# Which queue issues the projection's stores: ScalarE's or SyncE's, in an encoder layer with two kinds of attention

## The chip, the core and the metric

The kernel runs on one NeuronCore of a Trainium2 chip. The metric is the device time of one execution in microseconds. TensorE (PE) multiplies matrices, VectorE (DVE), ScalarE (ACT) and GpSimd (POOL) do the elementwise work, and SyncE (SP) computes nothing: its queue issues DMAs. Every engine takes its instructions in order; an instruction that waits holds all that stand behind it on the same engine.

## The reference

One layer on x of 2048 tokens by 1024 features, float32. A projection gives queries, keys and values of 16 heads of width 64, and 8 forget gates. Eight heads attend causally with a bias of summed log gates; eight attend within their own chunk of 64 tokens and the 8 chunks before, with a bias on clipped distance. The heads' outputs go through a second projection, are added to the input and normalised; then comes a feed-forward part with a causal convolution of width 3 and a gated GELU, and a second normalisation.

```python
proj = x @ w_in
q_a, k_a, v_a, f_a, q_b, k_b, v_b = jnp.split(proj, SPLITS, axis=-1)
y_a = forgetting_attention(split_heads(q_a, N_HEADS_A), split_heads(k_a, N_HEADS_A),
                           split_heads(v_a, N_HEADS_A), log_f)
y_b = chunked_band_attention(split_heads(q_b, N_HEADS_B), split_heads(k_b, N_HEADS_B),
                             split_heads(v_b, N_HEADS_B), rel_bias)
...
x = layer_norm(DEEPNORM_ALPHA * x + mix, ln1_g[l], ln1_b[l])
u = x @ w_up
u = sum(u_pad[:, j:j + s, :] * conv_w[j] for j in range(CONV_WIDTH)) + conv_b
value, gate = jnp.split(u, 2, axis=-1)
return (value * jax.nn.gelu(gate)) @ w_down
```

## The kernel before

Dense products are made of three matmuls each (`mm3`, lines 184 to 186): an operand is split into a high part that the matmul unit represents and a low part that is the rest (`split`, ACT at line 177 and VectorE or GpSimd at line 180). The products of the feed-forward part go by sums and differences of blocks, seven products in place of eight, so their weights have to be summed and split too.

There are four stages. First the projection (`projection`): for each pair of heads `p`, for queries and for keys, and for each of four chunks of 512 tokens, `queries_or_keys` accumulates eight products of 128 by 512, ScalarE writes the high part (line 419), VectorE the low part (line 420), and both are stored to DRAM (lines 423 and 424). `values` does the same for four heads at a time, in blocks of 128 tokens: ScalarE copies the sum (line 399), line 400 stores it. Each of the two functions hands back control after every product of three matmuls: 1024 such units in all, 8 to each of the 128 results.

Attention reads these arrays back. A unit of attention is one head and one chunk of 512 queries. `load_keys` loads kb, ka and vv (lines 514 to 523), `maxima` loads qa and qb (lines 552 to 554, two buffers each), multiplies them (`sc`, line 574), takes maxima on VectorE (lines 577 and 582), and ScalarE copies their transposed row into qb (line 592). `logits` then multiplies again (`st`, lines 611 and 612), ScalarE takes the exponential (line 623), and four steps later `weigh` multiplies by the values (`y`, line 698). The maxima of one unit are made while the unit before it is under way.

`weave` emits projection and attention in turn: so much dense work after each step of attention. Within the dense work, every ninth unit after the 60th takes one step of the generator `prepare_weights`. It loads raw tiles of the second projection's and of the last product's weights (`w_raw`, line 288), sums and splits them (`w_hl`, lines 279, 177, 180) and stores both parts (line 282), so that later stages load them ready. The raw tiles have one buffer each, and so has `w_hl`.

All DMAs are issued by SP. The second projection, the normalisation (until about 1460 us) and the feed-forward part follow.

Of the kernel before, what the change touches and what calls it, by code (L numbers as in the profile page):

```python
# [25 lines left out]
CH = 512  # L26
# [53 lines left out]
    ((7,), (), ((0, 1), (1, 1))),  # L80
)

PRE0, PRE = 60, 9
AHEAD_L, AHEAD_P, RESERVE = 5, 2, 16
DLY_V, DLY_R, DLY_Z = 32, 16, 16
WNEXT = 3
# [13 lines left out]
def f32(ap):  # L100
    return ap.bitcast(F32)
# [3 lines left out]
def hymba_layer(  # L105
# [18 lines left out]
    nc = tc.nc  # L124

    def tl(pool, shape, dt, tag, bufs=None):
        return pool.tile(shape, dt, tag=tag, name=tag, bufs=bufs)
# [46 lines left out]
    def split(hi, lo, src, hi_eng, lo_eng):  # L174

        if hi_eng is nc.scalar:
            nc.scalar.activation(hi, src, AF.Copy)  # L177
        else:
            hi_eng.tensor_copy(hi, src)
        lo_eng.tensor_tensor(lo, src, f32(hi), op=ALU.subtract)  # L180

    def mm3(acc, wh, wl, mh, ml, first, last, **more):

        nc.tensor.matmul(acc, wh, mh, start=first, stop=False, **more)  # L184
        nc.tensor.matmul(acc, wh, ml, start=False, stop=False, **more)  # L185
        nc.tensor.matmul(acc, wl, mh, start=False, stop=last, **more)  # L186
# [57 lines left out]
    def part(ws, k):  # L244
        ks = slice(k % (KT // 2) * P, (k % (KT // 2) + 1) * P)
        return [w[:, ks] for w in ws[k // (KT // 2)]]
# [24 lines left out]
    def prepare_weights(pool):  # L271

        def parts(dst, u, v=None, op=None):
            hl = tl(pool, [P, 2, CH], F32R, "w_hl")
            if v is not None:
                src = f32(hl[:, 1])
                nc.vector.tensor_tensor(src, u, v, op=op)
                u = src  # L280
            split(hl[:, 0], hl[:, 1], u, nc.scalar, nc.vector)
            nc.sync.dma_start(dst.rearrange("l p m -> p l m"), f32(hl))

        def load(src, tiles):
            raws = []
            for n, (i, j) in enumerate(tiles):
                raws.append(tl(pool, [P, CH], F32, f"w_raw{n}"))
                nc.sync.dma_start(raws[n], src[i * P : i * P + P, CH * j : CH * j + CH])
            return raws

        for k in range(0, KT, 2):
            tiles = [(k + n // 2, n % 2) for n in range(4)]
            raws = load(w_out, tiles)
            yield
            for raw, (i, j) in zip(raws, tiles):
                yield
                parts(wo_d[i, j], raw)
        HF = NF // 2
        for k in range(HF):
            raws = load(w_down, [(HF * i + k, j) for i in range(2) for j in range(2)])  # L300
            yield
            for n in DOWN:
                yield
                (k0, l0), v, op = DOWN[n][3:6]
                parts(wd_d[k, n], raws[2 * k0 + l0], v and raws[2 * v[0] + v[1]], op)


    def projection(mem, banks, state):
# [3 lines left out]
        def flush():  # L312
            while pending:
                pending.pop(0)()
# [9 lines left out]
        def gates(c, f):  # L324

            z, u, e, l = (tl(small, [P, TQ, 8], F32, f"gate{n}") for n in range(4))
            nc.vector.tensor_tensor(z, f, bf_t, op=ALU.add)
            nc.vector.scalar_tensor_tensor(u, z, -1.0, z, op0=ALU.mult, op1=ALU.min)
            nc.scalar.activation(e, u, AF.Exp)
            nc.vector.tensor_scalar(u, e, 1.0, None, op0=ALU.add)  # L330
            nc.scalar.activation(l, u, AF.Ln)

            nc.vector.scalar_tensor_tensor(e, u, -1.0, e, op0=ALU.add, op1=ALU.subtract)
            nc.vector.reciprocal(u, u)
            nc.vector.tensor_mul(e, e, u)
            nc.vector.tensor_sub(l, l, e)

            nc.vector.scalar_tensor_tensor(l, z, 0.0, l, op0=ALU.min, op1=ALU.subtract)
            nc.vector.tensor_scalar(l, l, -1.0, None, op0=ALU.mult)
            pending.append(lambda: sums_of_gates(c, l))  # L340
# [42 lines left out]
        def values(g, chunks, vs):  # L383
            nv = 264 if g == 0 else 256
            for c in chunks:
                if g == 0:
                    f = tl(small, [P, TQ, 8], F32, "f", 2)
                for t in range(TQ):
                    o = slice(t * P, t * P + P)
                    acc = banks.get()  # L390
                    for k in range(KT):
                        mm3(acc[:, :nv], *(x[:, o] for x in xs[k, c]), *vs[k], k == 0, k == KT - 1)
                        yield 0.33
                    if t == 1:
                        flush()
                    if g == 0:
                        nc.vector.tensor_copy(f[:, t], acc[:, 256:264])
                    tile = mem.get()
                    nc.scalar.activation(tile[:, :256], acc[:, :256], AF.Copy)
                    nc.sync.dma_start(  # L400
                        v_d[4 * g : 4 * g + 4, :, TQ * c + t, :].rearrange("h p d -> p h d"),
                        tile[:, :256].rearrange("p (h d) -> p h d", d=HD),
                    )
                    mem.put(tile, delay=DLY_E)
                if g == 0:
                    gates(c, f)
            mem.put(*held)
            held.clear()

        def queries_or_keys(p, j, c, ws):  # L410
            hd, ld = ((qh_d, ql_d), (kh_d, kl_d))[j]
            acc = banks.get()
            for k in range(KT):
                mm3(acc, *part(ws, k), *xs[k, c], k == 0, k == KT - 1)
                yield 0.65
            flush()
            hi, lo = mem.get(F32R), mem.get(F32R)
            sc = SCALE if j == 0 else 1.0
            nc.scalar.activation(hi, acc, AF.Copy, scale=sc)
            nc.vector.scalar_tensor_tensor(  # L420
                lo, acc, sc, f32(hi), op0=ALU.mult, op1=ALU.subtract
            )
            nc.sync.dma_start(hd[p, :, c * CH : (c + 1) * CH], f32(hi))
            nc.sync.dma_start(ld[p, :, c * CH : (c + 1) * CH], f32(lo))
            mem.put(hi, lo, delay=DLY_E)

# [2 lines left out]
        for half in range(2):  # L429
# [8 lines left out]
            for g in range(4):  # L438
                for p in (2 * g, 2 * g + 1):
                    if half == 0 and p == 0:  # L440

                        ahead = None
                        for c in chunks:
                            for j in range(2):
                                if (j, c) == (1, 1):
                                    mem.put(*sum(first[0], ()))
                                    ahead = weights(w_qk[1, 0], mem)
                                yield from queries_or_keys(p, j, c, first[j])
                        mem.put(*sum(first[1], ()))
                        continue  # L450
                    for j in range(2):
                        ws = ahead or weights(w_qk[p, j], mem)
                        if (p % 2, j) == VAT:
                            vs = value_weights(g, state.pop("early", None))
                        ahead = None
                        if len(mem.free) >= WFREE + (20 if (p % 2, j) < VAT else 0):
                            ahead = weights(w_qk[(2 * p + j + 1) // 2 % NP, (j + 1) % 2], mem)
                        for c in chunks:
                            yield from queries_or_keys(p, j, c, ws)
                        mem.put(*sum(ws, ()))  # L460
                        if (p % 2, j) == VPOS:
                            yield from values(g, chunks, vs)
# [750 lines left out]
    with ExitStack() as st:  # L1213
# [75 lines left out]
        with ExitStack() as inner:  # L1289
            state["weights"] = prepare_weights(inner.enter_context(tc.tile_pool(name="w_s", bufs=1, side="right")))  # L1290
            with tc.tile_pool(name="v_s", bufs=1, side="right") as state["early"]:
                projected(1)
            pools = attention_pools(inner)
            weave(attention(pools, [0, 1], lambda p: projected(p // 2 + 1)), dense, RATE1)
            weave(attention(pools, [2, 3], lambda p: projected(4 + p // 2 + 1)), dense, RATE2)
# [98 lines left out]
```

## Time and profile before

| | |
|---|---|
| median of 3 runs | 2788.2 us (2786.32 to 2790.31) |
| the profiled execution | 2789.79 us, span 2788.0 us |
| mean granted clock of TensorE | 0.993 |
| busy share of the span: TensorE, VectorE, ScalarE, GpSimd | 98%, 70%, 42%, 22% |

The span reaches from the first to the last instruction of the profiled execution. Times in views are us from the span's start. A wait is given with the instruction that waits, what released it, the sum of such waits, their number and the longest one. "PEld" is TensorE's load of the stationary operand, which runs beside the matmul before it; "q" after an engine's name means its queue of issues and waits.

### The profile page before, as it was taken

Reading aid. Unit: us, or ns where it says so; the run is one execution under the profiler, and the core shown is the slowest. Engines: PE = TensorE matmul, PEld = TensorE weight load, DVE = VectorE, ACT = ScalarE, POOL = GpSimd, SP = SyncE. Lnnn points to the kernel's source line nnn. Section 1 sums busy time; section 2 is a strip of 40 time slices with the busy share of each in tenths; the row PEclk is TensorE's granted clock in tenths of the full one; section 3 lists DMA queues with packets and bytes.
Section 4 is the critical chain, followed back from the end, with each engine's and each line's share of the span. In section 5 each row is a group of like instructions: output and inputs, shape, how many; then the busy total and the mean of one; then the engine's idle time right before and its main releaser. Section 6 shows DMA issues by size and latency. Waiting matters only on the chain.

```text
span 2788.0 us, 38642 instructions
## 1 busy us (share of the span) xinstructions
PE 2724.5 (98%) x12632; PEld 2045.3 (73%) x12632; DVE 1941.7 (70%) x3577; ACT 1160.7 (42%) x2004; POOL 623.2 (22%) x754
## 2 busy tenths in 40 slices
PE   9999999999999999999998999999999999999998
PEld 7676767675666656766786888888887788888886
DVE  4557576777677655668568888876568877777559
ACT  4434444444444443433225555553222555544221
POOL 2235242327567555333000000000000000000000
PEclk9999999999999999999999999999999999999999
DMA  8666767665455444677894444428778222236974
GB/s 242 197 207 196 228 194 229 211 201 169 144 182 182 137 144 153 199 198 217 293 328 142 141 166 156 155 83 311 260 247 322 87 80 81 78 88 206 323 227 161
DMA packets 324618, 527.40 MB, mean 189 GB/s; under 512 B 70688, under 2 KB 86176, under 8 KB 324416
## 3 DMA queue, kind: packets, MB, share of 16 engines
q1 hardware_dynamic: 324416, 524.93, 59.1%
q8 instruction: 100, 1.64, 0.2%
q14 instruction: 102, 0.84, 0.1%
HBM read 362.65 MB, written 162.14 MB: 188 GB/s over the span
## 4 chain that ended last, share of the span: by engine, by line
PE 84%; DVE 4%; DMA 4%; ACT 1%; issue 1%; POOL 0%; SPq 0%; DVEq 0%; ACTq 0%; POOLq 0%
PE acc L184 21%; PE acc L186 21%; PE acc L185 21%; PE y L698 8%; PE st L611 4%; PE sc L574 4%; PE st L612 3%; DMA qb<-qh_d 1%; PE sc L650 1%; DVE slot L180 1%; DVE slot L1132 1%; DMA slot<-in_w_v_dram 1%; DMA wd_d<-w_hl 1%; PE acc L841 0%; DVE slot L816 0%
## 5 line engine op out<-in xcount | busy, mean ns | idle before, releaser
L184 PE MATMUL acc<-slot,slot 128*128 128x512 f32 (+2 forms) x3064 | 1165.7, 381 | 17.9 <-ACT slot L177 17.9
L186 PE MATMUL acc<-slot,slot 128*128 128x512 f32 (+2 forms) x3064 | 1160.5, 379 | 6.6 <-DVE slot L180 6.6
L185 PE MATMUL acc<-slot,slot 128*128 128x512 f32 (+2 forms) x3064 | 1161.3, 379 | 0.0
L177 ACT ACTIVATE slot<-slot 128x512 fp32r<-128x512 f32 (+1 forms) x680 | 416.4, 626 | 674.2 <-DVE slot L1121 193.0
L184 PEld LDWEIGHTS acc<-slot,slot 128*128 128x128 f32 x3064 | 580.4, 189 | 135.9 <-ACT slot L177 23.5
L186 PEld LDWEIGHTS acc<-slot,slot 128*128 128x128 f32 x3064 | 579.7, 189 | 126.2 <-DVE slot L180 10.8
L185 PEld LDWEIGHTS acc<-slot,slot 128*128 128x128 f32 x3064 | 580.4, 189 | 112.6 <-issue 2.8
L180 DVE TENSOR_TENSOR slot<-slot,slot 128x512 fp32r<-128x512 f32 (+1 forms) x652 | 450.7, 707 | 194.4 <-ACT slot L177 167.9
L632 POOL TENSOR_TENSOR sums<-sums,pt 128x512 f32<-128x512 f32 (+3 forms) x416 | 426.0, 1024 | 251.9 <-ACT pt L623 189.0
L623 ACT ACTIVATE pt<-st 128x512 f32<-128x512 f32 (+3 forms) x544 | 261.7, 492 | 333.4 <-PE st L612 121.4
L698 PE MATMUL y<-pt,vv 128*64 128x512 f32 (+3 forms) x1088 | 281.6, 505 | 0.2 <-DVE yt L640 0.2
L611 PE MATMUL st<-qa,ka 128*128 128x512 f32 (+2 forms) x544 | 209.0, 385 | 9.0 <-ACT pt L623 8.5
L574 PE MATMUL sc<-kb,qb 66*128 66x512 f32 (+2 forms) x544 | 186.6, 373 | 10.8 <-DMA qb<-qh_d 8.1
L612 PE MATMUL st<-qb,kb 97*128 97x512 f32 (+2 forms) x544 | 189.9, 357 | 4.4 <-ACT qb L592 3.9
L577 DVE TENSOR_REDUCE mx<-sc 128x1 f32<-128x512 f32 x192 | 127.9, 686 | 80.0 <-PE sc L574 78.3
L611 PEld LDWEIGHTS st<-qa,ka 128*128 128x128 f32 x544 | 103.0, 189 | 96.0 <-issue 44.1
L698 PEld LDWEIGHTS y<-pt,vv 128*64 128x64 f32 x1088 | 82.0, 136 | 124.2 <-issue 111.5
L574 PEld LDWEIGHTS sc<-kb,qb 66*128 66x128 f32 x544 | 99.5, 190 | 78.6 <-DVE mx L582 17.5
L856 DVE SCALAR_TENSOR_TENSOR v<-u,cw,v 128x1024 f32<-128x1024 f32 x88 | 113.0, 1285 | 62.4 <-ACT v L855 44.2
L1005 POOL COPY u<-halo 128x2 f32<-128x2 f32 x44 | 17.6, 401 | 620.8 <-DVE v L857 620.8
L582 DVE CUSTOM_DVE_ANT_0 junk<-sc,bq 128x512 bf16<-128x512 f32 (+2 forms) x224 | 108.2, 483 | 49.4 <-PE sc L574 40.2
L632 POOL TENSOR_TENSOR sums<-pt 128x384 f32<-128x384 f32 (+1 forms) x64 | 79.5, 1243 | 255.4 <-PE sc L650 181.4
(116 smaller groups left out, 2250.3 us busy)
## 6 DMA issues: line engine op xcount, KB each, us to landing
slot<-wd_d SPq DMA_DIRECT2D x308, 256.0 KB
slot<-in_w_up_dram SPq DMA_DIRECT2D x176, 256.0 KB
wd_d<-w_hl SPq DMA_DIRECT2D x77, 512.0 KB
slot<-wo_d SPq DMA_DIRECT2D x128, 256.0 KB
h_d<-v SPq DMA_DIRECT2D x44, 512.0 KB
slot<-h_d SPq DMA_DIRECT2D x88, 256.0 KB
slot<-in_w_qk_dram SPq DMA_DIRECT2D x66, 256.0 KB
xq_d<-slot SPq DMA_DIRECT2D x56, 256.0 KB
```

Source lines behind the costliest of these rows:

```text
L177: nc.scalar.activation(hi, src, AF.Copy)
L180: lo_eng.tensor_tensor(lo, src, f32(hi), op=ALU.subtract)
L184: nc.tensor.matmul(acc, wh, mh, start=first, stop=False, **more)
L185: nc.tensor.matmul(acc, wh, ml, start=False, stop=False, **more)
L186: nc.tensor.matmul(acc, wl, mh, start=False, stop=last, **more)
L574: nc.tensor.matmul(sc[:, m0:m1], qb[:KR, tq], kb[:KR, m0:m1], start=True, stop=True)
L577: nc.vector.tensor_reduce(m, sc[:, k0:k1], axis=AX.X, op=ALU.max)
L611: nc.tensor.matmul(st[:, w2], ka[:, js], qa[:, w2], start=True, stop=False)
L612: nc.tensor.matmul(st[:, w2], kb[:KM, js], qb[:KM, w2], start=False, stop=True)
L623: nc.scalar.activation(pt[:, w], st[:, w], AF.Exp)
L632: nc.gpsimd.tensor_tensor(acc[:, w], (acc if first is None else first)[:, w], pt[:, w], op=ALU.add)
L698: nc.tensor.matmul(y[half, w], v, pt[:, w], start=first and n < 2, stop=last and n >= len(tiles) - 2)
```

## The change

The stores of high parts (line 423) and of values (line 400) are issued by ScalarE's queue in place of SP's. In `prepare_weights`, a group of raw tiles is loaded after one more step of the generator, and the generator takes a step every 8 units in place of 9. The store of low parts (line 424), the loads and all arithmetic stay as they were.

```diff
-PRE0, PRE = 60, 9
+PRE0, PRE = 60, 8
...
         for k in range(0, KT, 2):
             tiles = [(k + n // 2, n % 2) for n in range(4)]
+            yield
             raws = load(w_out, tiles)
             yield
...
         for k in range(HF):
+            yield
             raws = load(w_down, [(HF * i + k, j) for i in range(2) for j in range(2)])
             yield
...
                     nc.scalar.activation(tile[:, :256], acc[:, :256], AF.Copy)
-                    nc.sync.dma_start(
+                    nc.scalar.dma_start(
                         v_d[4 * g : 4 * g + 4, :, TQ * c + t, :].rearrange("h p d -> p h d"),
...
-            nc.sync.dma_start(hd[p, :, c * CH : (c + 1) * CH], f32(hi))
+            nc.scalar.dma_start(hd[p, :, c * CH : (c + 1) * CH], f32(hi))
             nc.sync.dma_start(ld[p, :, c * CH : (c + 1) * CH], f32(lo))
```

## Rows read from the trace of the kernel before

**Rows 1.** The page, busy time of the engines (share, instructions).
```profile
PE 2724.5 (98%) x12632; PEld 2045.3 (73%) x12632; DVE 1941.7 (70%) x3577; ACT 1160.7 (42%) x2004; POOL 623.2 (22%) x754
```
**Rows 2.** Busy time by stage; last: granted clock, DMA share, GB/s.
```profile
94.00:1180.00 1086.00, 1062.15 (x5332) 726.86 (x5331) 704.49 (x1622) 473.13 (x933) 501.62 (x511) 0.99 0.61 185
...
1460.00:2788.00 1328.00, 1302.00 (x5606) 1050.32 (x5604) 1008.54 (x1410) 566.68 (x842) 45.98 (x128) 0.99 0.53 175
```
**Rows 3.** What TensorE's matmuls waited for, 94 to 1180 us: sum, number, longest.
```profile
PE sc L574 <- DMA qb<-qh_d: 8.1, 8, 2.1
PE st L611 <- ACT pt L623: 6.4, 7, 2.1
PE st L612 <- ACT qb L592: 3.9, 3, 2.8
```
**Rows 4.** Busy time around two long waits, and in a stretch between.
```profile
130.00:160.00 30.00, 27.18 (x133) 19.54 (x131) 19.54 (x40) 12.35 (x24) 15.79 (x15) 0.94 0.59 180
160.00:340.00 180.00, 179.79 (x972) 131.41 (x972) 106.65 (x241) 76.06 (x154) 61.92 (x67) 1.00 0.71 214
...
740.00:780.00 40.00, 37.87 (x205) 27.03 (x205) 22.78 (x41) 16.28 (x31) 20.22 (x17) 0.96 0.41 129
```
**Rows 5.** What SP's queue waited for, 0 to 1180 us.
```profile
SPq L423 <- ACT slot L419: 87.3, 47, 6.8
SPq L400 <- ACT slot L399: 69.7, 47, 8.4
SPq L552 <- PE st L612: 59.3, 28, 7.9
...
SPq L424 <- DVE slot L420: 18.3, 32, 2.4
SPq L288 <- DVE w_hl L279: 17.0, 9, 3.5
```
**Rows 6.** The issues of lines 423 and 400, 94 to 1180 us: ns min/median/max, first and last start.
```profile
L423 SPq DMA_DIRECT2D kh_d<-slot x28: 320/327/808, 113.8 to 1178.7; - x28
...
L400 SPq DMA_DIRECT2D v_d<-slot x56: 359/376/539, 160.5 to 1159.6; - x56
```
**Rows 7.** SP's issues in order of time, 744 to 754 us: start, duration.
```profile
745.25 0.38 SPq L400 DMA_DIRECT2D v_d<-slot  x1
...
750.93 0.45 SPq L552 DMA_DIRECT2D qa<-ql_d  x1
...
752.61 0.55 SPq L554 DMA_DIRECT2D qb<-qh_d  x1
```
**Rows 8.** What SP's queue waited for, 745 to 754 us.
```profile
SPq L400 <- ACT slot L399: 8.4, 1, 8.4
SPq L552 <- PE st L612: 3.4, 1, 3.4
SPq L230 <- DMA v_d<-slot: 1.5, 1, 1.5
```
**Rows 9.** A high part, qb's copy and the logits in order of time, 229 us.
```profile
229.29 0.60 ACT L419 ACTIVATE slot<-acc 128x512 fp32r<-128x512 f32 x1 [3.30 <-PE acc L186]
...
229.98 0.59 ACT L592 ACTIVATE qb<-sc 1x512 fp32r<-1x512 f32 x1
...
230.62 0.30 PEld L612 LDWEIGHTS st<-qb,kb 97*128 97x128 f32 x2 [0.25 <-ACT qb L592]
```
**Rows 10.** ScalarE's groups, 94 to 1180 us: busy, mean ns, idle before, releasers.
```profile
L623 ACT ACTIVATE pt<-st 128x512 f32<-128x512 f32 (+1 forms) x468 | 229.5, 501 | 278.2 <-PE st L612 113.8 <-DVE st L621 72.0 <-DVE st L618 57.2
...
L592 ACT ACTIVATE qb<-sc 1x512 fp32r<-1x512 f32 x55 | 32.2, 586 | 45.4 <-PE sc L591 44.9
```
**Rows 11.** What TensorE's weight loads waited for, 94 to 1180 us.
```profile
PEld st L611 <- ACT pt L623: 30.0, 54, 2.5
...
PEld st L612 <- ACT qb L592: 10.3, 16, 3.3
```
**Rows 12.** The stores of prepared weights: ns min/median/max, first and last start.
```profile
L282 SPq DMA_DIRECT2D wd_d<-w_hl x77: 359/377/1182, 208.5 to 1020.1; - x77
```

## The prediction

> **What bounds the kernel now.** I read the page first, then a table by stage, then who waited for whom on TensorE, on SP's queue and on ScalarE, and last the order of single instructions around a store. The page shows TensorE busy for 2724.5 of 2788.0 us [rows 1]: it idles 63.5 us in all, and whatever the other engines and queues do is worth time only where it makes or ends one of those idle stretches. The diff touches the projection, which is woven with attention, and the weight preparation that runs inside it. By stage, that is the stretch from 94 to 1180 us (and the 94 us before it): there TensorE is busy 1062.15 of 1086 us, so 23.85 us are idle; from 1460 us on nothing is touched [rows 2]. The waits that TensorE names in this stretch are 8.1 us for the load of qb (8 times), 6.4 us for an exponential on ScalarE (7 times) and 3.9 us for ScalarE's copy into qb (3 times) [rows 3]; these three are 18.4 of the 23.85 us. The rest is small waits for VectorE and GpSimd, and gaps too short for a releaser.
>
> A long idle stretch costs twice. Around the 2.8 us wait of 130 to 160 us [rows 3, 4] the granted clock is 0.94 of 2.4 GHz on the mean, in the quiet stretch after it 1.00, around the 2.1 us wait for qb at 758 us it is 0.96 [rows 4]. 0.06 of 30 us is 1.8 us, 0.04 of 40 us is 1.6 us: each stall of about 2 us cost about 1.7 us more in clock. Five such dips lie between 94 and 1200 us (two are shown), some 8.7 us by that price. So everything that the change can win in its stretch is some 24 us of idle time and 9 us of clock, 1.2% of the span; a measurable gain needs a sixth of it. For this kernel 0.2%, 5.6 us, is about what a measurement can tell from no change.
>
> **The stores, seen from SP.** 128 issues leave SP's queue: 64 of high parts, 64 of values. In the stretch they are 55 and 56, and one takes 0.327 or 0.376 us on the queue [rows 6] (the 27 stores of qh_d repeat the row of kh_d). SP also stops waiting for ScalarE: 87.3 us before high parts, 69.7 us before values, nearly all that these waits amount to [rows 5]. What is late next?
>
> For high parts nearly nothing is won. The low part's store stands right behind, stays on SP, and waits for a VectorE instruction that itself reads the high part; SP waits for it 18.3 us now, after having waited for the high part, and will wait the whole time then. Only the 0.33 us of issue comes free. I cost this at nothing; its cover is the low part's wait, and without that cover it would be a share of the next item.
>
> For values SP does get free, 69.7 us earlier in sum. Behind them on SP stand the loads of the next attention unit, of weights, and the stores of prepared weights. The stretch before the 2.1 us stall at 758 us is the test, as the longest wait of a value store lies in it: SP waited 8.4 us for ScalarE and issued the store at 745.25; but the load of qa, the first of the three loads that the unit needs, then waited another 3.4 us for a matmul of the unit before, that still read the buffer, and went out at 750.93, qb at 752.61 [rows 7, 8]. The store was gone 5 us before; without it the load goes out at 750.93 all the same. Of SP's waits before qa, 59.3 us, in 28 waits, are for that matmul [rows 5]. So the three loads are held by TensorE's own order and by the buffer, not by the stores. Bounds: nothing, and all of the 8.1 us for qb with the two clock dips at such stalls (1.8 and 1.6), 11.5 us. I take 1 us, one of the eight waits at their mean, near the lower end since the row that should show the link shows the other cause.
>
> By the Trainium skill, page Perfetto Trace Analysis, section DMA Optimizations, one engine may be given the inputs and another the outputs "to allow more dynamic spread"; by it the loads would start earlier, and the sum would go toward the 11.5 us. The row at 745 to 753 us speaks against it for this kernel [rows 7, 8], and no run before shows two issuing engines.
>
> **The stores, seen from ScalarE.** No DMA is issued by ScalarE before, so the nearest rows are the same issues on SP: 55 x 0.327 + 56 x 0.376 = 39 us of ScalarE's queue in the stretch, on an engine that is busy 473 of 1086 us there [rows 2, 6]. What stands behind the store on ScalarE is the next exponential, the copy into qb, or a split of a weight. At 229 us the copy into qb starts 0.09 us after the high part's copy ends, and the weight load of the logits waits for it [rows 9]: an issue in between goes straight to TensorE, 0.33 us.
>
> How often is that so? 468 exponentials and 55 copies into qb feed the logits [rows 10], and 54 + 16 = 70 times the weight load of the logits waited for one of them, 40.3 us [rows 11]: 13% of the 523 end just when they are needed. If each of the 111 stores delays one such instruction, 111 x 0.13 = 15 hits of about 0.35 us are 5.2 us: the upper end. Of the 40.3 us of weight-load waits only 10.3 us are waits of the matmul itself [rows 3]; the rest ran beside a matmul under way. With that share, 0.26, the hits cost 1.4 us: the lower end. I take 3 us, between them: not every store delays an exponential, but the case at 229 us is a full hit. A gain is excluded here: ScalarE gets work and loses none.
>
> **Raw tiles one step later, a step every 8 units.** Each group of four loads now comes after one more step, so the generator has 4 x 6 + 11 x 9 = 123 steps where it had 4 x 5 + 11 x 8 = 108; 1024 - 60 units of the projection give 107 turns every 9 and 120 every 8. The same 93 parts are prepared with the same instructions, at nearly the same pace. SP's waits before the raw loads (17.0 us for VectorE [rows 5]) shrink. No matmul of this stretch reads these weights; the work that hides them is the projection itself: the last store of prepared weights goes out at 1020.1 us and the last key store at 1178.7 [rows 6, 12]. A delay of up to 158 us is covered. If that cover were gone, the three or four steps left at the end would run in one burst, against one or two. I take nothing, with the same bounds as SP's share above.
>
> **Sum.** 2789.79 us was the profiled execution's own time, span 2788.0. +3 on ScalarE, -1 on SP, 0 for the raw tiles: 2791.8. The median of the runs, 2788.2, is 1.6 us below that execution, so 2790 us is what I expect of a median: 0.1% slower, inside what can be told from no change.
>
> **The rivals.**
> *Likeliest, 0.43: a wash.* As summed, 2783 to 2794.
> *SP's freedom reaches TensorE, 0.26: faster.* The loads of qb land earlier at half of the eight waits (4 us) and the two long ones drop below the length at which the clock fell (3.4 us): 2788.2 - 7.4 = 2781. For it speak 69.7 us of SP's waits before value stores, and 17.0 before raw tiles; against it the waits for TensorE behind them, 59.3 us [rows 5], and the case at 745 us. It decides from three or four of the eight on. The page's rule on inputs and outputs is this rival.
> *ScalarE becomes the late one, 0.31: slower.* All 15 hits come at full price, 5.2 us, and three stalls for an exponential or for qb's copy grow into the length that cost clock, 3 x 1.8: 10.6 us, 2799. For it speak that ScalarE already ends 10.3 us of TensorE's waits, and that an issue can also be held by an earlier DMA's landing (1.5 us for a load of w_qk at line 230 [rows 8]), which would then hold the exponentials too; against it that ScalarE idles 56% of the stretch. It decides from the first dip more than before.
> *The change does nothing to the queue* is not a separate case: low parts hold SP as long as high parts did, which is in the sum.
>
> **Numbers.** Faster by over 0.2% (below 2782.6): 0.25, nearly all of the second case. Within: 0.44. Slower (above 2793.8): 0.31. The likeliest case alone is 2783 to 2794; the range reaches into both others, whose centres are 2781 and 2799, to 2778 and 2801: beyond lie the bound of 11.5 us of gain, and more than three added dips.
>
> **What the profile of the changed kernel would show.** SP's waits at the stores of high parts and values are gone; its wait at the low part's store grows from 18.3 us toward 90. If the sum is right, TensorE idles 24 to 28 us from 94 to 1180 us, its waits for ScalarE (10.3 us) grow by 1 to 5, its waits for qb stay within 2 us of 8.1, and the clock is below 0.97 in about as many places. Faster is right if the waits for qb fall below 5 us and the dip at 740 to 780 us is gone. Slower is right if ScalarE's next instruction after a store is what the logits wait for, with more than 15 us of such waits. The prediction is wrong if the engines' orders come out so different that stalls move to other tiles, POOL's sums or VectorE's maxima, by more than 5 us: then the balance of two queues was not the question.

## The result, and the profile after

The changed kernel takes 2805.9 us (median of 8 runs, 2795.9 to 2809.3) against 2787.0 us (2783.5 to 2791.9). The ratio on record is 1.0056, 95% interval 1.0043 to 1.0068; the two medians alone would give 1.0068, its upper end. It is slower, and the median is past the upper end of the predicted range, 2801. The profiled execution spans 2807.5 us. Lines beyond 300 moved by two: the logits are lines 613 and 614, the high part's copy and store 421 and 425, the value's 401 and 402, the low part's store 426, qb's load 556.

The page of the changed kernel, busy time and DMA queues (packets, MB, share of 16 engines); busy time by stage; what TensorE's matmuls waited for from 94 to 1180 us; what SP's queue waited for from 0 to 1180 us; and the two moved stores from 94 to 1180 us (ns min/median/max, first and last start):

```profile
PE 2728.3 (97%) x12632; PEld 2045.0 (73%) x12632; DVE 1934.1 (69%) x3577; ACT 1162.8 (41%) x2004; POOL 620.6 (22%) x754
...
q1 hardware_dynamic: 281408, 499.76, 55.7%
q10 hardware_dynamic: 43008, 25.17, 2.9%
```
```profile
94.00:1180.00 1086.00, 1051.76 (x5230) 715.31 (x5230) 685.22 (x1589) 461.61 (x911) 494.01 (x505) 0.99 0.57 178
1460.00:2788.00 1328.00, 1310.27 (x5645) 1056.78 (x5644) 1004.50 (x1400) 570.90 (x846) 44.86 (x128) 0.99 0.54 177
```
```profile
PE sc L576 <- DMA qb<-qh_d: 13.1, 20, 1.4
PE st L613 <- ACT pt L625: 7.9, 11, 1.5
PE sc L576 <- DVE mx L584: 5.2, 1, 5.2
PE sc L652 <- POOL sums L634: 2.6, 1, 2.6
PE st L614 <- ACT qb L594: 2.1, 3, 1.3
```
```profile
SPq L282 <- DVE w_hl L180: 103.2, 48, 9.0
SPq L426 <- DVE slot L422: 64.4, 37, 7.9
SPq L554 <- PE st L614: 60.4, 24, 8.8
...
SPq L525 <- DMA v_d<-slot: 20.2, 8, 4.1
```
```profile
L425 ACTq DMA_DIRECT2D qh_d<-slot x28: 326/327/353, 95.5 to 1129.4; - x28
```
```profile
L402 ACTq DMA_DIRECT2D v_d<-slot x55: 366/367/431, 160.6 to 1177.4; - x55
```

The stores did move: queue 10, which the kernel before does not use, carries 25.17 MB, and an issue takes 0.327 or 0.367 us on ScalarE, nearly as it did on SP [rows 6]. TensorE is busy 1051.76 of 1086 us from 94 to 1180 us, so it idles 34.2 us where it idled 23.9 [rows 2]. Over the whole span the same 12632 matmuls are busy 3.8 us longer (2728.3 against 2724.5 [rows 1]), so 15.7 of the 19.5 us between the two spans are idle time. From 94 to 1180 us the waiting for qb grew most, from 8.1 us (8 times) to 13.1 (20 times) [rows 3]. One stall for a maximum on VectorE is 5.2 us long, and one for sums on GpSimd 2.6; in the kernel before the same two waits were:

```profile
PE sc L574 <- DVE mx L582: 2.4, 2, 1.2
PE sc L650 <- POOL sums L632: 1.4, 1, 1.4
```

The waits for ScalarE's exponentials and copies into qb, where the price was expected, are 10.0 us, after 10.3. SP waits for low parts 64.4 us (18.3 before [rows 5]), for VectorE's prepared weights 103.2 us (57.3 before), and for landings of the moved stores 71.0 us in 33 waits, all rows that name kh_d, qh_d or v_d as written summed, where it was 13.1 us in 13. Two of these rows in the kernel before:

```profile
SPq L282 <- DVE w_hl L180: 57.3, 28, 7.8
...
SPq L523 <- DMA v_d<-slot: 2.6, 2, 1.9
```

Where the time went can be read by counting exponentials: the 101st of the 544 starts 3.4 us later than before, the 141st 12.4, the 201st 17.4, the 321st 21.3, the last 18.4 us. So the loss is made while attention runs beside the projection, mostly between 345 and 640 us, and little comes on top later. That stretch, first in the changed kernel, then in the kernel before:

```profile
345.00:640.00 295.00, 279.29 (x1434) 197.70 (x1433) 200.98 (x532) 125.33 (x261) 95.71 (x135) 0.98 0.65 199
```
```profile
345.00:640.00 295.00, 286.48 (x1491) 203.72 (x1489) 214.32 (x554) 133.18 (x273) 101.25 (x134) 1.00 0.70 210
```

VectorE and ScalarE get less done there too: all wait more, and the granted clock is 0.98 in place of 1.00. These are two single executions, and the runs of the kernel before lie up to 8.4 us apart, so a difference of a few us in such rows can be chance.

One thing had not been in the prediction's sum. The order in which instructions stand on an engine's queue is not that of the code: a planner fixes it when the kernel is built. Taking 128 stores off SP changes that plan on other engines too. In the two traces that differ only in who issues the stores (the changed kernel and e1_raw_only below), of 120 splits into slots on ScalarE (mostly weights and tokens, line 177) that stand among the exponentials 63 stand further ahead and 7 further behind, 2.7 exponentials earlier on the mean; of 88 splits of prepared weights 87 stand earlier, 15 exponentials on the mean.

One such place. ScalarE's order in the changed kernel, with TensorE's beside it, and below them the same split (the third and the fourth exponential are the same ones too) in e1_raw_only:

```profile
367.69 1.08 ACT L625 ACTIVATE pt<-st 128x512 f32<-128x512 f32 x2 [0.98 <-DVE st L620]
370.88 0.63 ACT L177 ACTIVATE slot<-slot 128x512 fp32r<-128x512 f32 x1 [2.10 <-DMA qh_d<-slot]
371.42 0.54 ACT L625 ACTIVATE pt<-st 128x128 f32<-128x128 f32 x2
```
```profile
370.00 0.28 PE L614 MATMUL st<-qb,kb 97*128 97x256 f32 x1
371.73 0.45 PE L613 MATMUL st<-qa,ka 128*128 128x384 f32 x1 [1.45 <-ACT pt L625]
```
```profile
356.93 1.09 ACT L625 ACTIVATE pt<-st 128x512 f32<-128x512 f32 x2
358.34 0.28 ACT L625 ACTIVATE pt<-st 128x128 f32<-128x128 f32 x1 [0.32 <-PE st L614]
359.43 0.63 ACT L177 ACTIVATE slot<-slot 128x512 fp32r<-128x512 f32 x1 [0.81 <-DMA qh_d<-slot]
359.96 0.75 ACT L625 ACTIVATE pt<-st 128x256 f32<-128x256 f32 x2
```

In e1_raw_only three exponentials are done before the split. In the changed kernel two are; the split then waits 2.10 us until an earlier store has left the slot that it writes, the third exponential waits behind it, and TensorE idles 1.45 us. No store stands between them.

### The profile page after: what moved, and what is told of

Its sections match the earlier page's. It is cut to its first block, busy times and chain, and to the rows that moved or that the text cites. A ratio compares the mean times of both kernels' runs of the same rounds, so it can differ in the third digit from the quotient of the medians.

```text
span 2807.5 us, 38622 instructions
## 1 busy us (share of the span) xinstructions
PE 2728.3 (97%) x12632; PEld 2045.0 (73%) x12632; DVE 1934.1 (69%) x3577; ACT 1162.8 (41%) x2004; POOL 620.6 (22%) x754
## 3 DMA queue, kind: packets, MB, share of 16 engines
q10 hardware_dynamic: 43008, 25.17, 2.9%
## 4 chain that ended last, share of the span: by engine, by line
PE 83%; DMA 8%; DVE 4%; ACT 2%; issue 1%; SPq 1%; POOL 0%; ACTq 0%; DVEq 0%; POOLq 0%
PE acc L186 21%; PE acc L184 21%; PE acc L185 21%; PE y L700 8%; PE sc L576 4%; PE st L613 4%; DMA qb<-qh_d 3%; PE st L614 3%; PE sc L652 1%; DVE slot L180 1%; DMA slot<-in_w_qk_dram 1%; DMA slot<-y_d 1%; DVE slot L1134 1%; DMA qh_d<-slot 1%; DVE slot L818 1%
## 5 line engine op out<-in xcount | busy, mean ns | idle before, releaser
L180 DVE TENSOR_TENSOR slot<-slot,slot 128x512 fp32r<-128x512 f32 (+1 forms) x652 | 444.0, 698 | 203.7 <-ACT slot L177 173.3
L700 PE MATMUL y<-pt,vv 128*64 128x512 f32 (+3 forms) x1088 | 275.9, 507 | 0.0
L658 DVE RECIPROCAL row<-row 128x128 f32<-128x128 f32 x128 | 115.6, 928 | 27.0 <-ACT row L654 26.9
```

The costliest lines, as they stand in the source:

```text
L700: nc.tensor.matmul(y[half, w], v, pt[:, w], start=first and n < 2, stop=last and n >= len(tiles) - 2)
```

## The experiments

Three theories. **ScalarE:** its time for the issues delays exponentials (the prediction's +3 us). **SP:** set free, it runs on into other waits and issues other transfers at other times, and loads come late. **Order:** the new plan of all engines is the loss, whoever issues the stores. Times are ratios to the kernel before on the same chip, with 95% intervals. The expectations use letters: A is a part of the SP theory (loads held by the landing of stores), B lays the loss on the raw tiles' new pace, C is ScalarE, D is order; "queue theories" are SP and ScalarE together. Where two edits are alike, only one of them is printed.

### One part alone

**e1_raw_only**: the raw tiles and the step of 8, the stores left on SP.
```diff
-PRE0, PRE = 60, 9
+PRE0, PRE = 60, 8
...
+            yield
             raws = load(w_out, tiles)
...
```


> Only the raw tiles' extra step and the step every 8 units; all stores stay on SP. Theory A (the stores are the cause: loads that SP could reach earlier are held by the landing of stores that ScalarE issues later): 2787 us, within 4 us of the kernel before, waits for qb near 8 us. Theory B (the prepared weights' new pace, with everything reordered by it, is the cause): 2800 to 2808 us.


Measured 1.0005 [0.9991, 1.0019]: the raw tiles cost nothing that can be measured.

**e2_hi_only**: only the high parts' stores on ScalarE. **e3_v_only**: only the values'. **e4_both_stores**: both, with the raw tiles as before.
```diff
-            nc.sync.dma_start(hd[p, :, c * CH : (c + 1) * CH], f32(hi))
+            nc.scalar.dma_start(hd[p, :, c * CH : (c + 1) * CH], f32(hi))
```


> Only the high parts' stores on ScalarE. Theory A: half of the loss, 2793 to 2800 us. Theory B: 2787 us, within 4 us of before. Theory C (ScalarE's own 0.35 us for each issue delays the exponentials and the copies into qb): about half of the loss too, but with the added idle time at those two, not at the loads of qb.

> Only the values' stores on ScalarE. Theory A: more than half of the loss, 2795 to 2803 us, with SP's waits for the landing of value stores above 50 us (72 us with the whole change, 15 before). Theory B: 2787 us, within 4 us. Theory C: about half of the loss, at the exponentials.

> Both stores on ScalarE, the prepared weights as before. Theory A and theory C: nearly the whole loss, 2800 to 2808 us. Theory B: 2787 us, within 4 us.


Measured 1.0109 [1.0092, 1.0126], 1.0080 [1.0065, 1.0095] and 1.0114 [1.0097, 1.0132]. Either half costs nearly what both cost: no sum over stores does that, neither ScalarE's time per issue nor SP's freedom per store. And e4_both_stores with the raw tiles later is the changed kernel, 1.0056: the raw tiles, which cost nothing alone, give half of the loss back. TensorE's waits in e2_hi_only, 94 to 1180 us:

```profile
PE st L611 <- ACT pt L623: 15.3, 14, 2.4
PE sc L574 <- DMA qb<-qh_d: 11.5, 14, 2.4
```

Against 6.4 and 8.1 us before, both grew, and mostly not after stores: of the 20 gaps of TensorE (21.0 us, before 1220 us) that an exponential or qb's copy ended, four (3.3 us) have a store's issue on ScalarE within the 2.5 us before the gap's end.

### First attempts at the queues

**f1_double**: SP keeps all stores; ScalarE also stores the same tiles to a place that nobody reads.
```diff
             nc.sync.dma_start(hd[p, :, c * CH : (c + 1) * CH], f32(hi))
+            nc.scalar.dma_start(h2_d[j, p, :, c * CH : (c + 1) * CH], f32(hi))
```


> SP keeps all its stores as before, and ScalarE issues the same 128 stores again, into scratch arrays that nobody reads: ScalarE bears the whole of its new work (some 45 us of issues), 25 MB more are moved, and the weights' splits stand in ScalarE's order where they stood before (mean shift 0.0 and -0.7 exponentials). Theory C (ScalarE's time for the issues): 2805 to 2822 us. Theory D (with the stores off SP, the order made for the engines puts the weights' splits 3 to 17 exponentials earlier on ScalarE, and there they wait for loads that on the chip land no earlier, with the exponentials held behind them): within 6 us of 2788.


1.0178 [1.0155, 1.0202]. ScalarE's order is nearly that of before, but 25 MB more move, so this did not separate what it was meant to.

**f2_pool**: GpSimd issues the stores (`nc.gpsimd.dma_start` in both places).


> The same two stores off SP, but issued by GpSimd. ScalarE issues nothing; the splits stand as early as with the stores on ScalarE (2.9 and 17.8 exponentials). Theory C: within 6 us of 2788, or the loss is on GpSimd's sums. Theory D: 2805 to 2822 us, with TensorE's added waits at the exponentials, the copy into qb and the loads of qb.


1.0187 [1.0168, 1.0206]. Nothing is issued by ScalarE, and the loss is greater. But GpSimd takes longer for an issue:

```profile
L423 POOL DMA_DIRECT2D qh_d<-slot x28: 540/557/567, 94.6 to 1155.8; - x28
```
```profile
L400 POOL DMA_DIRECT2D v_d<-slot x50: 750/767/775, 160.6 to 1170.1; - x50
```

and its queue holds attention's sums and the low parts of the values' weights behind the stores, so this too is mixed. ScalarE's order shifts as in e4_both_stores.

**f3_sp_later**: the stores stay on SP, and the code emits them some units of the projection later, so that SP should not have to wait for ScalarE.
```diff
+                if k == LATE:
+                    write()
```


> All stores stay on SP but are emitted three units after their result, so that SP no longer waits for ScalarE and VectorE before them; the splits keep their places (0.0 and 0.0). The rival that forecast a gain from SP's freedom: 2776 to 2783 us. Theory D: SP's freedom is worth little by itself, 2782 to 2790 us, with SP's waits before the stores down from 175 us to under 60.


1.0005 [0.9993, 1.0017], but SP's waits before the stores stayed, 81.9 and 72.4 us (87.3 and 69.7 before [rows 5]): a later place in the code did not make SP issue them later. The attempt says nothing on what SP's waits are worth; it shows that the order on the queue is not the order of the code.

**f4_late_weights**: e4_both_stores with the prepared weights begun later.
```diff
-PRE0, PRE = 60, 9
+PRE0, PRE = 150, 8
```


> Both stores on ScalarE; the prepared weights begin 90 units later and then take a step every 8 units, which puts their splits back to about where they stood (-2.1 exponentials for -16.9), while the splits of the projection's own weights stay 3.1 early. Theory D: a third or more of the loss of 32 us is gone, 2797 to 2810 us. Theory C: 2815 to 2822 us as with both stores on ScalarE.


1.0110 [1.0088, 1.0131]: with the splits of prepared weights back near their old places among the exponentials (2.6 earlier on the mean, 19.2 in e4_both_stores), the loss is the same, as the ScalarE theory would have it. Their early place is not the cause.

### ScalarE's time and issues alone

**g1_act_time**: a second copy of 128x256 behind each of the 128 copies. **g2_tiny**: a store of one row by ScalarE behind each. SP keeps all stores; the order stays nearly as before. The first adds copies that nobody reads, the second 128 small transfers.
```diff
             nc.scalar.activation(hi, acc, AF.Copy, scale=sc)
+            nc.scalar.activation(idle, f32(hi)[:, :256], AF.Copy)   # g1_act_time
+            nc.scalar.dma_start(t_d[j, p, c], f32(hi)[0:1])         # g2_tiny
```


> Stores stay on SP; ScalarE gets, right behind each of the 128 copies, another copy of 128x256 into a tile that nobody reads (0.38 us each by the row of the value copy, 49 us in all, about the time of the 128 issues). It adds ScalarE's time without a DMA. The prediction's price for ScalarE's time: +1.4 to +5.2 us, 1.0005 to 1.002. If ScalarE's time is the whole loss of e4_both_stores: 1.008 to 1.013. If it costs nothing: 0.999 to 1.001.

> Stores stay on SP; ScalarE also issues, behind each of the 128 copies, a store of one row (1 or 2 KB) of the same tile to a place that nobody reads: the same number of issues, order of the engines nearly as before, hardly any bytes. If the issue on ScalarE with its queue's own handling is the loss: 1.008 to 1.013. If f1_double (1.0178) lost by its 25 MB of added traffic and by landings: 1.000 to 1.004.


0.9990 [0.9977, 1.0003] and 0.9988 [0.9978, 0.9998]. In g1_act_time ScalarE (the fourth busy time) is busy 512.72 us where it was 473.13 [rows 2], and TensorE, the first, loses 2 us of busy time in that window:

```profile
94.00:1180.00 1086.00, 1060.14 (x5322) 724.70 (x5321) 706.83 (x1621) 512.72 (x1042) 499.75 (x511) 0.99 0.61 185
```

The ScalarE theory falls as an account of the loss: 40 us more work, or 128 more issues, cost nothing that can be measured. The order was not held here, only nearly kept, so a gain by a slightly other plan could hide a loss of 0.1 or 0.2%.

### The order held

`add_manual_dep` with NoSync ties an instruction behind another of its own engine without a wait. With one such edge between each two neighbours, the five queues can be given the order that another kernel has (all but the moved stores, which the planner places):
```python
for a, b in zip(names, names[1:]):          # one engine's instructions, in the wanted order
    tc.add_manual_dep(
        by[b], a,
        mybir.DependencyInfo(mybir.DependencyClass.NoSync, mybir.DependencyReason.DATA),
        reason="order",
    )
```
**h1_order_alone**: stores on SP, all queues in the order of e4_both_stores. **h2_queue_alone**: stores on ScalarE, all queues in the order of the kernel before. **i1_after_order** and **i2_after_queue**: the same two for the changed kernel and e1_raw_only.

> Stores stay on SP as in the kernel before, but every engine's instructions (on SP: all but the moved stores) are held, by edges that order and do not wait, in the order that they have in e4_both_stores (1.0114). Order theory (the plan that the two queues bring about, with splits of weights earlier on ScalarE, ahead of exponentials, is the loss): 1.008 to 1.014, waits for exponentials and for qb together 25 us or more. Queue theories (the loss is in what the queues do at run time: SP free to walk into other waits, landings of stores on another queue, ScalarE's issue time): 0.998 to 1.004, the two waits together under 20 us.

> Both stores on ScalarE as in e4_both_stores, but every engine's instructions (on SP: all but the moved stores) are held in the order that they have in the kernel before. Order theory: 0.997 to 1.003, the waits for exponentials and qb together back at 13 to 20 us. Queue theories: 1.008 to 1.014 with 25 us or more of the two waits; ScalarE's issue time at the price of the prediction alone (+3 us, at most 5.2): 1.000 to 1.002.

> The change itself in place of e4_both_stores: raw tiles as in the changed kernel, stores on SP (e1_raw_only: 1.0005), every engine's instructions held in the order that they have in the changed kernel. Order theory: 1.006 to 1.014, waits for exponentials and qb together 22 us or more; theory of two about equal causes, order and queue, in the changed kernel (1.0056): 1.002 to 1.005; queue alone: 0.998 to 1.002.

> The changed kernel (stores on ScalarE, raw tiles later), with every engine's instructions held in the order that they have in e1_raw_only, where the stores are on SP. Order theory: 0.998 to 1.002; order and queue about equal causes, as h2_queue_alone (1.0043) has it: 1.002 to 1.005; queue alone: 1.005 to 1.008, as in the changed kernel, with qb waits near its 13.9 us.

| order planned for | raw tiles | stores on SP | stores on ScalarE |
|---|---|---|---|
| stores on SP | as before | 1 (the kernel before) | 1.0043 [1.0027, 1.0058] h2_queue_alone |
| stores on ScalarE | as before | 1.0174 [1.0154, 1.0195] h1_order_alone | 1.0114 [1.0097, 1.0132] e4_both_stores |
| stores on SP | later | 1.0005 [0.9991, 1.0019] e1_raw_only | 1.0043 [1.0029, 1.0057] i2_after_queue |
| stores on ScalarE | later | 1.0102 [1.0084, 1.0120] i1_after_order | 1.0056 [1.0043, 1.0068] the changed kernel |

h1_order_alone lies above its range for the order theory (1.008 to 1.014), h2_queue_alone between all its ranges, i1_after_order in the range for order (1.006 to 1.014), i2_after_queue in that for two about equal causes (1.002 to 1.005).

The order alone, with not one store moved, costs 1.0 to 1.7%. Part of that may be a misfit: SP then carries the stores in an order that was planned without them. TensorE's waits in i1_after_order from 94 to 1180 us, and there the place shown above, ScalarE and then TensorE (the exponential is line 1021, the split 573):

```profile
PE st L1009 <- ACT pt L1021: 14.5, 17, 3.0
PE sc L972 <- DMA qb<-qh_d: 11.5, 15, 2.2
PE sc L972 <- DVE mx L980: 5.9, 1, 5.9
PE st L1010 <- ACT qb L990: 5.1, 7, 1.7
```
```profile
378.86 1.09 ACT L1021 ACTIVATE pt<-st 128x512 f32<-128x512 f32 x2 [0.98 <-DVE st L1016]
381.51 0.63 ACT L573 ACTIVATE slot<-slot 128x512 fp32r<-128x512 f32 x1 [1.56 <-DMA qh_d<-slot]
382.05 0.53 ACT L1021 ACTIVATE pt<-st 128x128 f32<-128x128 f32 x2
```
```profile
382.36 0.44 PE L1009 MATMUL st<-qa,ka 128*128 128x384 f32 x1 [0.90 <-ACT pt L1021]
```

The same split stands ahead of the same exponential, waits 1.56 us, and TensorE idles 0.90 us, with every store on SP. The columns are not a sum, though. In the new order ScalarE is the better queue for the stores (1.0102 to 1.0056), in the old order it is the worse one (to 1.0043). With the stores on ScalarE, giving the old order back wins 0.7% in e4_both_stores; in the changed kernel 0.13%, and the intervals overlap. That is also how the raw tiles "gave back" half: with the old orders held both versions cost 1.0043, so with the raw tiles later the plan for stores on ScalarE is a better plan.

### What is left with the order held

**m1_hi_queue**, **m2_v_queue**: e2_hi_only and e3_v_only in the order of the kernel before.

> Only the high parts' stores on ScalarE, every engine's order held as in the kernel before. With the order free the same edit gave 1.0109 (e2_hi_only). The prediction's own step (low parts hold SP as long as high parts did): 0.999 to 1.001. If the 1.0043 that is left in h2_queue_alone comes from SP's new waits for ScalarE's landings and for low parts in equal shares: 1.002 to 1.003. If order was not the cause for this part: 1.009 to 1.013.

> Only the values' stores on ScalarE, every engine's order held as in the kernel before. With the order free the same edit gave 1.0080 (e3_v_only). If what is left in h2_queue_alone comes from values, whose slots are loaded again while the store has not landed (waits of up to 12.4 us there): 1.003 to 1.005. Equal shares: 1.002 to 1.003. If order was not the cause for this part: 1.006 to 1.010.


1.0011 [0.9995, 1.0026] and 1.0021 [1.0006, 1.0036]. With the order held the halves add up (0.32% against 0.43%, inside the intervals), and most of 1.0109 and 1.0080 goes when the old order is given back.

**n3_sp_keeps_waits**: h2_queue_alone, and where SP issued a store it now issues one row of the same tile.
```diff
-            nc.sync.dma_start(hd[p, :, c * CH : (c + 1) * CH], f32(hi))
+            nc.sync.dma_start(t_d[j, p, c], f32(hi)[0:1])
+            nc.scalar.dma_start(hd[p, :, c * CH : (c + 1) * CH], f32(hi))
```


> Both stores on ScalarE and every engine's order held as in the kernel before (as h2_queue_alone, 1.0043), but where SP issued them it now issues a store of one row (1 or 2 KB) of the same tile to a place that nobody reads: SP keeps its waits for ScalarE and its issues, the bytes go through ScalarE's queue. If the remaining 0.43% comes from SP's freedom (it runs on into other waits and issues other transfers earlier): 0.998 to 1.002. If it comes from ScalarE's queue with its bytes and landings: 1.003 to 1.006.


1.0015 [1.0003, 1.0026]. What SP waited for (0 to 1180 us; line 676 or 680 stores prepared weights, 818 or 824 low parts) and what qb cost TensorE (94 to 1180 us), first in h2_queue_alone, then here:

```profile
SPq L676 <- DVE w_hl L574: 93.0, 39, 7.7
SPq L818 <- DVE slot L814: 83.7, 39, 7.7
```
```profile
SPq L624 <- DMA v_d<-slot: 12.4, 1, 12.4
```
```profile
PE sc L968 <- DMA qb<-qh_d: 12.3, 13, 2.1
```

```profile
SPq L822 <- ACT slot L818: 84.2, 49, 6.8
SPq L798 <- ACT slot L797: 68.0, 47, 8.7
SPq L680 <- DVE w_hl L578: 65.5, 31, 7.7
...
SPq L824 <- DVE slot L819: 22.1, 34, 2.4
```
```profile
PE sc L974 <- DMA qb<-qh_d: 9.8, 12, 1.4
```

With its waits for ScalarE given back (84.2 and 68.0 us), SP waits for prepared weights 65.5 us in place of 93.0, for low parts 22.1 in place of 83.7, and for landings of the moved stores 27.5 us in 19 waits in place of 51.2 in 20; one wait of 12.4 us for the landing of a value, which held a load of a weight (line 624, there 628), is down to 0.8. The time falls from 1.0043 [1.0027, 1.0058] to 1.0015; the intervals just fail to overlap, and the two were measured on different chips. So of the 12 us (0.43% of 2788) some 8 come from SP running on, and some 4 (0.15%) are left for ScalarE's queue with its bytes; both figures are uncertain by several us. The profiled execution of n3_sp_keeps_waits is one of its fastest (2788.4 us, median 2796.6), so qb's 9.8 us may flatter it.

**n4_sp_double**: f1_double with the second copy issued by SP, and the order held.
```diff
+            nc.sync.dma_start(h2_d[j, p, :, c * CH : (c + 1) * CH], f32(hi))
```


> Stores on SP, and SP also issues the copy of each store that ScalarE issued in f1_double (25 MB more, 128 issues more on SP, about 45 us of its queue); every engine's order held as in the kernel before; nothing on ScalarE. If f1_double (1.0178) lost by the bytes alone: 1.014 to 1.022. If it lost by the bytes being on a second queue: under 1.010.


1.0263 [1.0246, 1.0281]: above both expectations. Adding 25 MB and, in the trace, 57 us of issues to SP costs more than adding 25 MB to ScalarE's queue, so a loss like f1_double's needs no second queue. With g2_tiny, where as many issues without the bytes cost nothing, that points to the bytes, or to slots that come free later because two stores read each of them; the two were not told apart. TensorE's waits, 94 to 1180 us:

```profile
PE st L1023 <- ACT pt L1035: 23.1, 18, 3.8
PE sc L986 <- DMA qb<-qh_d: 20.0, 17, 3.7
```

## Why the prediction was wrong

**What bounds the kernel: right in the main.** Nearly all of the loss is made before 1200 us, in the stretch named, and what grew most there, the load of qb, is one of the three waits named. TensorE's gaps after it are 22.7 us (from 1220 us on, as all comes some 20 us later), 21.2 before. The clock had the smaller part: busy time grew by 3.8 us, idle time by 15.7.

**The stores, seen from SP: this step failed.** It was costed at -1 us, with bounds from nothing to a gain of 11.5; a loss was not among them. It asked only whether loads would go out earlier. What the runs showed in its place is two losses that come with taking the stores off SP. First, with every queue's order as it was, the freed SP runs into waits for low parts, for prepared weights and for landings that its waits for ScalarE used to cover. With the stores on ScalarE and the old order held, the loss is 12 us in all (h2_queue_alone), and some 8 of them go when SP gets those waits back (n3_sp_keeps_waits). Second, the order does not stay: ScalarE's splits into slots move ahead of exponentials when the stores leave SP, whether they go to ScalarE (e4_both_stores, 2.6 on the mean) or to GpSimd (f2_pool, 2.8), and not when ScalarE issues stores while SP keeps its own (f1_double, 0.0). The new order costs 1.0% with every store on SP (i1_after_order). With the stores on ScalarE, as in the changed kernel, giving the old order back wins only 0.13%, inside the intervals (i2_after_queue). So either alone makes a loss, and neither alone can be undone to get the time back: the 0.56% can't be divided between them. The step's reading of 745 to 753 us was one place, and it took the order of all instructions for given. Its own sign, SP's wait for low parts growing toward 90 us, came only in part (64.4), while waits that it had not named grew: for landings by 58 us, for prepared weights by 46.

Within it, high parts were costed at nothing since the low part behind them would hold SP as long. With the order held that stands, 1.0011 [0.9995, 1.0026]; with the order free the same 64 stores cost 1.09%.

**Inputs and outputs on two engines.** By the Trainium skill, Perfetto Trace Analysis, DMA Optimizations, one engine may be given the inputs and another the outputs "to allow more dynamic spread". No run here shows a gain by it in the old order (1.0043 twice); in the order planned for two queues, stores on ScalarE do beat stores on SP (1.0102 to 1.0056, 1.0174 to 1.0114), and both stay behind the kernel before. The split was not whole, as SP kept the stores of low parts and of prepared weights.

**The stores, seen from ScalarE: the size not refuted, the mechanism not seen.** +3 us, bounds 1.4 to 5.2. The terms were read nearly rightly (55 issues at 0.327 us, 55 at 0.367 for 56 at 0.376), but the hits did not show: 40 us more work on ScalarE, or 128 issues of one row, measured -0.1%, and TensorE's waits for ScalarE did not grow (10.0 us, 10.3 before). The example at 229 us was no measure of how often. The 0.15% that n3_sp_keeps_waits leaves, some 4 us, is as large as the term; since bare issues cost nothing, that would be luck and not its reason.

**Raw tiles: right alone** (1.0005), but not independent: beside the moved stores they change the plan, and the loss is 0.56% in place of 1.14%.

**The rivals.** The slower one (ScalarE becomes the late one, 2799) had the sign and not the mechanism. The sentence on what would make the prediction wrong, orders so different that stalls move to GpSimd's sums or VectorE's maxima by more than 5 us, named the right cause; its sign came about at the limit (maxima 6.0 us after 2.4, sums 2.6 after 1.4, 4.8 us more in all), and as much went to qb (5.0). It carried no chance, and should have been a rival with a price.

What stays open: which of the moved instructions make the 1.0% of the order; the one place shown, 1.45 us, is an example and not a sum. The prepared weights' splits on ScalarE are excluded (f4_late_weights, in the version without the later raw tiles); giving SP's new order without the other engines', or theirs without SP's, was not tried. Nor was the place of the moved stores themselves held, and why 0.15% is left in n3_sp_keeps_waits was not followed up.

## What to carry to other kernels

Where a planner lays out the queues, moving an instruction to another queue is two changes: who issues it, and the order of everything. Hold the order with edges that do not wait, and each can be timed by itself, though the two need not add up. The waits that SP's queue lost here did not vanish: ask where a freed queue stands next, and whether what it then waits for (a landing, a slow producer) is worse than what it was waiting for. And count how often an added instruction really hits the critical engine before giving it a price: here an engine idle for over half of the stretch took 40 us more at no measurable cost.

## What the runs showed of the hardware that was not expected

An issue of the same store took 0.33 us (high part) on SP and on ScalarE alike, 0.38 and 0.37 us (value), and 0.56 and 0.77 us on GpSimd. 25 MB of added stores, in a kernel that moves 525 MB, cost 1.8% from ScalarE's queue (f1_double) and 2.6% from SP's (n4_sp_double), though the DMA engines' mean busy share in the stretch was only 0.70 and 0.68.
